# A decoder trunk on one core: turning the second layer's x token-major by transposing transfers of 16-bit halves

## The chip, the core and the metric

The kernel runs on one core of a Trainium2 chip. The core has five engines with in-order instruction queues: TensorE (PE, matrix products; its weight loads are shown apart as PEld), VectorE (DVE), ScalarE (ACT), GpSimd (POOL) and SyncE (SP), which here only issues transfers. Transfers run on 16 DMA engines, whichever queue issues them. The metric is the device time of one execution in microseconds; the smaller, the better.

## The reference

Two layers of a hybrid decoder trunk on x of shape (1, 512, 1024) in float32. Each layer adds two terms to x: the mixer (four gated branches, merged and projected by `w_out`) and a gated feed-forward network.

```
h = rmsnorm(x, norm_mix)
... four branches from h @ w_in, lifted, gated and summed: merged
x = x + merged @ w_out
hf = rmsnorm(x, norm_ffn)
gate, up = split(hf @ ffn_w_up, 2)
x = x + (silu(gate) * up) @ ffn_w_down
```

The change concerns the third line of the second layer. There x must exist in two layouts: with features on the partitions, for the products with `ffn_w_up`, and with tokens on the partitions, because the second layer's feed-forward output is accumulated onto x in that layout and written out.

## The kernel before

x lies feature-major: `xT` is a tile of 128 partitions x 8 feature chunks x 512 tokens. Every product is made from float32 values split into a high and a low part (`w_hi`, `w_lo`; `h_hi`, `h_lo`; `mg_hi`, `mg_lo`): three matmuls, at lines 320, 321 and 323, take the place of one. SP loads a piece of weights into `w_raw` (four buffers), ACT makes `w_hi` from it (three buffers, line 100, the helper `A` through which all ACT work goes), DVE makes `w_lo` (lines 257 and 1265). A matmul on a piece waits for both. A load is issued when a `w_raw` buffer is free.

`residual` (line 1178) forms `x + merged @ w_out`. It goes through the eight feature chunks m in four groups of two. In each group PE multiplies, and then for each m DVE adds the product to `xT[:, m, :]` (line 1193), `h_chunk` makes `h_hi`, `h_lo` and a square for the norm (lines 338 and 346 on DVE, line 100 on ACT), and the chunk is stored: in the first layer by a plain transfer of `xT` to `x_dram`, in the second layer by `turned(m)`. `turned` is the part that the change rewrites. Before, PE transposes four 128x128 blocks of the chunk into one PSUM tile `tr` (line 1181), ACT copies that tile to `xt` in SBUF, and a transfer on ACT's queue (line 1184) stores `xt` to `xt_dram` (`x_tokens` in the rows), which is laid out by tokens.

After `residual` comes `ffn`. Its first products, A11 and A12, take `h_hi` and `h_lo` directly. Line 1422 on DVE forms sums of them in a tile `acc`; a block of wide products follows (its loads at line 246). Then the accumulator `acc` is loaded by SP from `x_tokens` (`x_in`, line 1457), in two transfers, each after all stores to `x_tokens`. The last four PE transposes are kept in the list `last_turn`; `product` orders the second token tile's first matmul of A11 behind them.

The framework fixes the order of the instructions on each engine by a plan made before the run, in which urgent pieces (`w_hi`, `w_lo`) are taken first. On the chip each engine goes through its queue in that order and waits where an operand is not there yet. SBUF pools are freed and reused by tile: a later tile on the same place waits for the last user of the earlier one. `turned` takes its tiles from the pool `outp`, which holds `mg_hi`, `mg_lo` and two buffers of `xt`.

POOL meanwhile moves sums of the feed-forward weights through DRAM, one transfer after another (line 1280).

Of the kernel before, what the change touches and what calls it, by code (L numbers as in the profile page):

```python
# [12 lines left out]
F32 = mybir.dt.float32  # L13
F32R = mybir.dt.float32r
I32 = mybir.dt.int32
U8 = mybir.dt.uint8
AF = mybir.ActivationFunctionType
OP = mybir.AluOpType
AX = mybir.AxisListType
# [2 lines left out]
P = 128  # L22
S = 512
NT = S // P
# [47 lines left out]
def hybrid_trunk(ctx: ExitStack, tc: tile.TileContext, x, mem, positions, norm_mix, w_in, conv_w,  # L72
                 dsa_q_norm, dsa_k_norm, hgrn_lower_bounds, hgrn_out_norm, mem_norm, mem_w_kv,
                 mem_q_norm, mem_k_norm, w_lift, w_out, norm_ffn, ffn_w_up, ffn_w_down, out):
    nc = tc.nc
    act, dve, pe, pool = nc.scalar, nc.vector, nc.tensor, nc.gpsimd
# [11 lines left out]
    sync = mybir.DependencyInfo(mybir.DependencyClass.Sync, mybir.DependencyReason.DATA)  # L88
    tables = {AF.Exp: "natural_log_exp_and_others", AF.Ln: "natural_log_exp_and_others",
              AF.Silu: "silu_and_others"}  # L90
    table = {"set": None, "load": None, "users": []}

    def A(dst, src, func, **kw):
        name = tables.get(func)
        if name is not None and name != table["set"]:
            load = act.preload_act_table_set(name)
            for u in table["users"]:
                tc.add_manual_dep(load.ins, u.name, order, reason="table set")
            table.update(set=name, load=load.ins, users=[])
        i = act.activation(dst, src, func, **kw)  # L100
        if name is not None:
            tc.add_manual_dep(i.ins, table["load"].name, order, reason="table set")
            table["users"].append(i.ins)
        return i

    def mm_ps():
        return pmm.tile([P, 512], F32, name="mm")
# [4 lines left out]
    def tr_ps():  # L112
        return pat.tile([P, 512], F32, name="tr", bufs=TR_BUFS)

    def f(ap):
        return ap.bitcast(F32)

    consts.tile([P, 320], U8, name="spacer")
    ident = consts.tile([P, P], F32, name="ident")
# [17 lines left out]
                       base=0, channel_multiplier=1)  # L137
    future = consts.tile([P, P], U8, name="future")
    dve.tensor_scalar(future, causal_bias, 0.0, None, op0=OP.is_lt)
# [3 lines left out]
                       channel_multiplier=-1)  # L143
    tri = consts.tile([P, P], U8, name="tri")
    dve.tensor_copy(tri, tri_f)
    ps = tr_ps()
# [8 lines left out]
    warm = consts.tile([P, 1], F32, name="warm")  # L155
    A(warm, one, AF.Exp)
    mem_in = sp.tile([P, 2, D], F32, name="mem_in")
    for hf in range(2):
        c = slice(hf * D // 2, (hf + 1) * D // 2)
# [3 lines left out]
    ps = tr_ps()  # L163
    pe.transpose(ps[:, :KD], rows_m, ident[:KD, :KD])
    A(prm_m, ps[:, :KD], AF.Copy)
    N_ROWS = 70
    prm = consts.tile([P, N_ROWS], F32, name="prm")

    def parameters():
        ps = tr_ps()  # L170
        pe.transpose(ps[:, :N_ROWS], rows[:N_ROWS, :], ident[:N_ROWS, :N_ROWS])
        A(prm, ps[:, :N_ROWS], AF.Copy)

# [20 lines left out]
    for l in range(DEPTH):  # L194
        a = sp.tile([P, HD], F32, name=f"gq_raw{l}")
# [3 lines left out]
        b = consts.tile([P, HD], F32, name=f"gk{l}")  # L199
# [4 lines left out]
    def rstd(dst, ms, y, a):  # L204
        i = A(y, ms, AF.Ln, bias=eps[:, 0:1])
        A(y, y, AF.Exp, scale=-0.5, bias=half[:, 0:1])
        A(a, y, AF.Square, scale=2.0)
        dve.scalar_tensor_tensor(a, ms, EPS, a, op0=OP.add, op1=OP.mult)
        dve.scalar_tensor_tensor(dst, a, 3.0, y, op0=OP.subtract, op1=OP.mult, reverse0=True)
        return i  # L210
# [69 lines left out]
    def wchunk(src, kt, n):  # L280
        return Chunk(src, kt, n)
# [4 lines left out]
    def features(w, a, js, k0=0, kt=None, pss=None, made=None, late_lo=False):  # L286

        kt = w.kt if kt is None else kt
        pss = [mm_ps() for _ in js] if pss is None else pss
        runs = [(part, ks) for part in range(2) for ks, _, _ in w.parts] if late_lo else [(None, ks) for ks, _, _ in w.parts]  # L290
        for part, ks in runs:
            for j, ps in zip(js, pss):
                for k in ks:
                    last = mm3(ps, w.tile(k, j), pair(a, k0 + k), k0 + k == 0, k0 + k == kt - 1, part=part)[-1]
            if made is not None and (ks[-1] == w.kt - 1 or not late_lo):
                made.append(last)
        return pss
# [34 lines left out]
    def new_h():  # L332
        return (state.tile([P, KD, S], F32R, name="h_hi", bufs=1),
                state.tile([P, KD, S], F32R, name="h_lo", bufs=1))

    def h_chunk(h, ssq, c, gain, xs):
        A(h[0][:, c, :], xs, AF.Copy, scale=gain)
        dve.scalar_tensor_tensor(h[1][:, c, :], xs, gain, f(h[0][:, c, :]), op0=OP.mult, op1=OP.subtract)
        if ssq is None:
            return  # L340
        if c == 0:
            A(ssq, xs, AF.Square)
        else:
            sq = state.tile([P, S], F32, name="sq", bufs=2)
            A(sq, xs, AF.Square)
            dve.tensor_add(ssq, ssq, sq)
# [7 lines left out]
    def column_means(ps, ones, sq, hi, lo, scale=1.0):  # L354
        A(hi, sq, AF.Copy, scale=scale)
        dve.scalar_tensor_tensor(lo, sq, scale, f(hi), op0=OP.mult, op1=OP.subtract)
        return [pe.matmul(ps, ones, hi, start=True, stop=False), pe.matmul(ps, ones, lo, start=False, stop=True)]
# [3 lines left out]
    def norm_feature(ssq):  # L361
        ps = tr_ps()
        norm_mms.extend(column_means(ps, ones_hr, ssq, *(scratch512(S).bitcast(F32R) for _ in range(2)), scale=P / D))
        r = state.tile([P, S], F32, name="rstd", bufs=1)
        rstd(r, ps, scratch512(S), scratch512(S))
        return r
# [3 lines left out]
    def norm_token(ssq):  # L370
        ps = tr_ps()
        for t in range(NT):
            pe.matmul(ps[:, t:t + 1], ssq[:, t * P:(t + 1) * P], ones_d, start=True, stop=True)
        r = small(NT, name="rstd_t", bufs=2)
        after_split.append(rstd_into(r, ps[:, :NT], small, NT))
        return r
# [69 lines left out]
    h = new_h()  # L446
# [729 lines left out]
    last_turn = []  # L1176

    def residual(xT, w2d, a, kt, cols, h2, ssq2, gain, turn=None):
        def turned(m):
            ps = tr_ps()  # L1180
            last_turn[:] = [pe.transpose(ps[:, t * P:(t + 1) * P], xT[:, m, t * P:(t + 1) * P], ident) for t in range(NT)]
            xt = turn.tile([P, NT, P], F32, name="xt", bufs=2)
            A(xt, ps.rearrange("p (a b) -> p a b", b=P), AF.Copy)
            nc.scalar.dma_start(xt_dram[:, :, m * P:(m + 1) * P], xt)

        for m0 in range(0, KD, cols // P):
            w = wchunk(w2d[:, m0 * P:m0 * P + cols], kt, cols)
            pss = [mm_ps() for _ in range(cols // P)]
            for js in ([range(cols // P)] if m0 + cols // P < KD else [[j] for j in range(cols // P)]):
                features(w, a, js, 0, kt, [pss[j] for j in js])  # L1190
            for j in range(cols // P):
                m = m0 + j
                dve.tensor_add(xT[:, m, :], xT[:, m, :], pss[j])
                h_chunk(h2, ssq2, m, gain(m), xT[:, m, :])
                if turn is None:
                    nc.scalar.dma_start(x_dram[:, m, :], xT[:, m, :])
                else:
                    turned(m)
# [430 lines left out]
    for l in range(DEPTH):  # L1629
        with ExitStack() as ctx_mix:  # L1630
            h, ssq = mixer(l, h, (lambda: (norm_token(ssq), lambda: norm_feature(ssq))) if l else (lambda: norms), ctx_mix)
        h, ssq = ffn(l, h, ssq)
# [29 lines left out]
```

## Time and profile before

| | us |
|---|---|
| median of 3 runs | 1971.31 |
| lowest and highest run | 1971.04 and 1971.98 |
| span of the profiled execution, first to last instruction | 1969.1 |
| PE busy in that span | 1962.7 |
| stretch from the first chunk's addition of `residual` in the second layer (1598.78) to the last (1634.26) | 35.48 |

The profiled execution has no time of its own beside its span; 2.2 us of the median lie outside the span. PE's share of the span is 100%, and its granted clock is 2.4 GHz throughout (1.000 of full speed). DVE is busy for 75% and ACT for 60% of the span. An engine's busy time counts overlapped work of PE once; a matmul's duration runs from its start to its modelled end, while the next one has already started.

### The profile page before, as it was taken

To read this page: it belongs to the slowest core of one execution; us is meant where nothing else is said; L and a number is where in the kernel's file an instruction comes from. 1 tells how busy PE (TensorE), PEld (TensorE's weight loads), DVE (VectorE), ACT (ScalarE), POOL (GpSimd) and SP (SyncE) were. 2 spreads that over 40 slices of the span, in tenths; PEclk is the share of its full clock that TensorE was granted. 3 is DMA by queue.
4 is the path that set the end of the run, shared out by engine and by line. 5 is a ranking of instruction groups with operands and counts; after the bars stand their busy time and mean duration, and the time that the engine had idled before them with its cause. 6 is when DMAs were issued, how large, how long until landed. Compare 5 with 4: busy or idle time off the path is not lost.

```text
span 1969.1 us, 27206 instructions
## 1 busy us (share of the span) xinstructions
PE 1962.7 (100%) x9815; PEld 1646.4 (84%) x9815; DVE 1477.5 (75%) x2761; ACT 1182.0 (60%) x2038; POOL 235.6 (12%) x288
## 2 busy tenths in 40 slices
PE   9999999999999999999999999999999999999999
PEld 8898988878888888888889898888888888888887
DVE  7869997657776677776876889965678667867777
ACT  6653655866765456645655455477667656556464
POOL 1011111111111111100001111111111111111000
PEclk9999999999999999999999999999999999999999
DMA  8677667667777888886676766676677879888754
GB/s 303 204 173 172 166 166 173 154 146 173 170 190 207 226 234 266 241 237 191 198 223 162 177 150 168 160 181 152 165 176 171 210 196 253 254 263 239 213 185 138
DMA packets 224278, 385.27 MB, mean 196 GB/s; under 512 B 13194, under 2 KB 120272, under 8 KB 223888
## 3 DMA queue, kind: packets, MB, share of 16 engines
q1 hardware_dynamic: 165056, 244.16, 39.4%
q0 software_dynamic: 52192, 132.81, 32.9%
q10 hardware_dynamic: 6896, 6.58, 1.0%
q8 instruction: 77, 1.26, 0.2%
q14 instruction: 57, 0.47, 0.1%
HBM read 368.81 MB, written 140.51 MB: 259 GB/s over the span
## 4 chain that ended last, share of the span: by engine, by line
PE 100%; DVE 0%; ACT 0%; issue 0%; DVEq 0%; ACTq 0%
PE mm L320 24%; PE mm L321 24%; PE mm L323 24%; PE at L323 4%; PE at L320 4%; PE at L321 4%; PE tr L320 2%; PE tr L323 1%; PE tr L321 1%; PE at L838 1%; PE tr L878 1%; PE tr L867 1%; PE tr L1554 1%; PE at L837 1%; PE tr L804 0%; PE at L1136 0%
## 5 line engine op out<-in xcount | busy, mean ns | idle before, releaser
L100 ACT ACTIVATE w_hi<-w_raw 128x1024 fp32r<-128x1024 f32 (+1 forms) x435 | 457.5, 1054 | 350.8 <-PE mm L321 108.9
L320 PE MATMUL mm<-h_hi,w_hi 128*128 128x512 f32 x960 | 376.8, 394 | 0.0
L321 PE MATMUL mm<-h_lo,w_hi 128*128 128x512 f32 x960 | 376.8, 392 | 0.0
L323 PE MATMUL mm<-h_hi,w_lo 128*128 128x512 f32 x960 | 372.0, 393 | 0.0
L1265 DVE TENSOR_TENSOR w_lo<-w_raw,w_hi 128x1024 fp32r<-128x1024 f32 x211 | 256.2, 1217 | 130.1 <-ACT w_hi L100 129.3
L257 DVE TENSOR_TENSOR w_lo<-w_raw,w_hi 128x1024 fp32r<-128x1024 f32 (+1 forms) x224 | 272.0, 1216 | 78.6 <-ACT w_hi L100 76.7
L1280 POOL DMA_DIRECT2D up_sums<-in_ffn_w_up_dram x120 | 121.4, 1011 | 834.3 <-DMA up_sums<-in_ffn_w_up_dram 549.6
L320 PEld LDWEIGHTS mm<-h_hi,w_hi 128*128 128x128 f32 x960 | 180.4, 188 | 36.3 <-DVE zf L1053 0.8
L323 PEld LDWEIGHTS mm<-h_hi,w_lo 128*128 128x128 f32 x960 | 180.2, 188 | 36.3 <-issue 0.2
L321 PEld LDWEIGHTS mm<-h_lo,w_hi 128*128 128x128 f32 x960 | 180.4, 188 | 36.0
L321 PE MATMUL mm<-w_lo,h_hi 128*128 128x256 f32 (+2 forms) x568 | 187.6, 330 | 0.3 <-DVE w_lo L257 0.3
L323 PE MATMUL mm<-w_hi,h_lo 128*128 128x256 f32 (+2 forms) x568 | 187.7, 331 | 0.0
L320 PE MATMUL mm<-w_hi,h_hi 128*128 128x256 f32 (+2 forms) x568 | 181.4, 330 | 0.0
L321 PEld LDWEIGHTS mm<-w_lo,h_hi 128*128 128x128 f32 x568 | 107.7, 190 | 10.5 <-DVE w_lo L257 0.6
L323 PEld LDWEIGHTS mm<-w_hi,h_lo 128*128 128x128 f32 x568 | 107.7, 190 | 9.4
L320 PEld LDWEIGHTS mm<-w_hi,h_hi 128*128 128x128 f32 x568 | 107.4, 190 | 9.6 <-ACT w_hi L100 0.2
L1280 POOL DMA_DIRECT2D w_sums<-in_ffn_w_down_dram x66 | 62.2, 943 | 327.1 <-DMA w_sums<-in_ffn_w_down_dram 184.4
L100 ACT ACTIVATE prob<-prob,small 128x128 f32<-128x128 f32 (+3 forms) x128 | 68.8, 555 | 21.9 <-DVE small L853 16.3
L321 PE MATMUL mm<-y_lo,w_hi 128*128 128x512 f32 x192 | 75.7, 394 | 0.0
L320 PE MATMUL mm<-y_hi,w_hi 128*128 128x512 f32 x192 | 75.6, 395 | 0.0
L323 PE MATMUL mm<-y_hi,w_lo 128*128 128x512 f32 x192 | 75.3, 392 | 0.0
L100 ACT ACTIVATE gate_e<-gate 128x512 f32<-128x512 f32 x64 | 40.2, 628 | 41.9 <-DVE gate L661 41.3
(500 smaller groups left out, 4216.8 us busy)
## 6 DMA issues: line engine op xcount, KB each, us to landing
w_raw<-in_w_in_dram SPq DMA_DIRECT2D x144, 512.0 KB, 4.9
up_sums<-in_ffn_w_up_dram POOLq DMA_DIRECT2D x120, 512.0 KB, 7.0
w_raw<-up_sums SPq DMA_DIRECT2D x80, 512.0 KB, 5.1
w_raw<-in_ffn_w_up_dram SPq DMA_DIRECT2D x60, 512.0 KB, 4.8
w_sums<-in_ffn_w_down_dram POOLq DMA_DIRECT2D x54, 512.0 KB, 6.1
up_sums<-up_sums POOLq DMA_DIRECT2D x40, 512.0 KB, 5.0
w_raw<-in_w_lift_dram SPq DMA_DIRECT2D x32, 512.0 KB, 5.0
w_raw<-in_ffn_w_down_dram SPq DMA_DIRECT2D x24, 512.0 KB, 5.2
```

The lines of the kernel that those rows point to most:

```text
L100: i = act.activation(dst, src, func, **kw)
L257: i2 = dve.tensor_sub(lo, raw, f(hi))
L320: made += [pe.matmul(ps, ah, bh, start=first, stop=False, skip_group_check=more), pe.matmul(ps, ah, bl, start=False, stop=False, skip_grou ...
L321: pe.matmul(ps, ah, bl, start=False, stop=False, skip_group_check=more)]
L323: made += [pe.matmul(ps, al, bh, start=False, stop=last, skip_group_check=more)]
L837: return [pe.matmul(ps, q[:, hh, s], k[0][:, :n], start=True, stop=False), pe.matmul(ps, q[:, hh, s], k[1][:, :n], start=False, stop=True)]
L838: pe.matmul(ps, q[:, hh, s], k[1][:, :n], start=False, stop=True)]
L867: turn = pe.transpose(pp[:, (2 * e + i) * P:(2 * e + i + 1) * P], probs[2 * i + e][:, b * P:(b + 1) * P], ident)
L878: i = pe.matmul(pv[e * HD:(e + 1) * HD, c], vt[:, b, :], pt[:, b, e * 2 * P:(e + 1) * 2 * P], start=b == 0, stop=b == t)
L1265: two = A(hi, raw, AF.Copy), dve.tensor_sub(lo, raw, f(hi))
L1280: i = nc.gpsimd.dma_start(dst, src, **kw)
L1554: turns.extend(pe.transpose(ps[:, t * P:(t + 1) * P], us[t][:, j * P:(j + 1) * P], ident) for t in range(NT))
```

## The change

In the second layer's `residual`, the PE transposes and the copy out of PSUM go. In their place, for each chunk m:

- `halves_turned`: ACT copies the chunk, read as 16-bit numbers, into a tile `planes` so that all first halves of the 512 words lie ahead of all second halves (128 x 1024 numbers of 16 bits). Then SP issues one transposing transfer of `planes` (256 KB) into a tile `halves`, by blocks of 128 columns.
- `halves_joined`: ACT copies `halves` into `xt`, so that the two halves of each word lie together again (128 x 1024 numbers of 16 bits).

The store of `xt` on ACT's queue stays. `planes` and `halves` have two buffers of 2 KB per partition each, in the pool `outp`, which grows by 8 KB per partition. The list `last_turn` stays empty, so the order of A11's matmul behind the transposes goes too. Nothing else in the program is changed.

```diff
+    def halves_turned(src, planes, turned):
+
+        e = planes.bitcast(U16).rearrange("p (e c) -> p e c", e=2)
+        A(e, src.bitcast(U16).rearrange("p (c e) -> p e c", e=2), AF.Copy)
+        nc.sync.dma_start_transpose(turned.bitcast(U16).rearrange("p (b r) -> p b r", r=P), planes.bitcast(U16))
+
+    def halves_joined(dst, turned, blocks):
+
+        h = turned.bitcast(U16).rearrange("p (e b r) -> p e b r", e=2, r=P)[:, :, blocks, :]
+        A(dst.bitcast(U16).rearrange("p (b r e) -> p e b r", e=2, r=P), h, AF.Copy)
...
     def residual(xT, w2d, a, kt, cols, h2, ssq2, gain, turn=None):
         def turned(m):
-            ps = tr_ps()
-            last_turn[:] = [pe.transpose(ps[:, t * P:(t + 1) * P], xT[:, m, t * P:(t + 1) * P], ident) for t in range(NT)]
+            planes, halves = (turn.tile([P, S], F32, name=nm, bufs=2) for nm in ("planes", "halves"))
+            halves_turned(xT[:, m, :], planes, halves)
             xt = turn.tile([P, NT, P], F32, name="xt", bufs=2)
-            A(xt, ps.rearrange("p (a b) -> p a b", b=P), AF.Copy)
+            halves_joined(xt.rearrange("p a b -> p (a b)"), halves, slice(0, NT))
             nc.scalar.dma_start(xt_dram[:, :, m * P:(m + 1) * P], xt)
```

## Rows read from the trace of the kernel before

**Rows 1.** The page: span, busy time by engine, and chain by engine.
```profile
span 1969.1 us, 27206 instructions
...
PE 1962.7 (100%) x9815; PEld 1646.4 (84%) x9815; DVE 1477.5 (75%) x2761; ACT 1182.0 (60%) x2038; POOL 235.6 (12%) x288
...
PE 100%; DVE 0%; ACT 0%; issue 0%; DVEq 0%; ACTq 0%
```

**Rows 2.** All waits of PE, whole span: total us, times, longest us.
```profile
PE tr L148 <- DVE one L130: 1.2, 1, 1.2
PE mm L539 <- ACT w_hi L100: 0.7, 1, 0.7
PE mm L321 <- DVE w_lo L257: 0.3, 1, 0.3
```

**Rows 3.** Line 1181, the transposes: duration ns min/median/max, first and last start.
```profile
L1181 PE MATMUL tr<-ident,xT x32: 270/272/273, 1603.8 to 1637.6; 128*128 128x128 f32 x32
```

**Rows 4.** Timeline of PE around one chunk's transposes: start us, us, instruction.
```profile
1612.63 0.39 PE L321 MATMUL mm<-mg_lo,w_hi 128*128 128x512 f32 x1
1612.86 0.60 PE L1181 MATMUL tr<-ident,xT 128*128 128x128 f32 x4
...
1613.53 0.40 PE L320 MATMUL mm<-mg_hi,w_hi 128*128 128x512 f32 x1
```

**Rows 5.** Timeline of DVE: additions to x in layers one and two.
```profile
644.16 1.29 DVE L1193 TENSOR_TENSOR xT<-xT,mm 128x512 f32<-128x512 f32 x2 [3.35 <-PE mm L323]
...
1598.78 1.28 DVE L1193 TENSOR_TENSOR xT<-xT,mm 128x512 f32<-128x512 f32 x2 [3.35 <-PE mm L323]
...
1634.26 0.69 DVE L1193 TENSOR_TENSOR xT<-xT,mm 128x512 f32<-128x512 f32 x1 [0.63 <-PE mm L323]
```

**Rows 6.** Timeline of ACT: first evaluation of the wide block, layers one and two.
```profile
706.32 0.37 ACT L100 ACTIVATE fu<-at,rstd_t 128x128 f32<-128x128 f32 x1 [0.25 <-PE at L323]
...
1664.78 0.37 ACT L100 ACTIVATE fu<-at,rstd_t 128x128 f32<-128x128 f32 x1 [0.30 <-PE at L323]
```

**Rows 7.** Busy time between these marks: engines (instructions), clock, DMA share, GB/s.
```profile
644.16:706.32 62.16, 62.16 (x279) 51.57 (x278) 45.57 (x54) 34.58 (x45) 7.46 (x8) 1.00 0.86 229
1598.78:1664.78 66.00, 66.00 (x311) 54.76 (x310) 45.55 (x54) 39.05 (x53) 8.03 (x9) 1.00 0.87 230
```

**Rows 8.** Timeline of ACT at the end of the second layer's residual.
```profile
1637.89 0.60 ACT L100 ACTIVATE xt<-tr 128x512 f32<-128x512 f32 x1 [1.19 <-PE tr L1181]
...
1639.29 1.06 ACT L100 ACTIVATE w_hi<-w_raw 128x1024 fp32r<-128x1024 f32 x1 [0.79 <-PE mm L323]
```

**Rows 9.** Timeline of DVE behind that.
```profile
1640.38 1.23 DVE L1265 TENSOR_TENSOR w_lo<-w_raw,w_hi 128x1024 fp32r<-128x1024 f32 x1 [2.77 <-ACT w_hi L100]
1641.52 4.62 DVE L1422 TENSOR_TENSOR acc<-h_hi,h_lo 128x1024 f32<-128x1024 f32 x4
1646.06 1.22 DVE L257 TENSOR_TENSOR w_lo<-w_raw,w_hi 128x1024 fp32r<-128x1024 f32 x1
```

**Rows 10.** Timeline of PE: the matmul that uses this last low part.
```profile
1647.55 0.40 PE L321 MATMUL at<-w_lo,h_hi 128*128 128x512 f32 x1
```

**Rows 11.** Line 1184, the stores of xt: issue in ns; us from issue to landing.
```profile
L1184 ACTq DMA_DIRECT2D x_tokens<-xt x8: 520/521/669, 1605.1 to 1638.5; - x8
...
DMA to landing us min/median/max: 4.8/6.8/9.8
```

**Rows 12.** The page's DMA queues: packets, MB, share of 16 engines (q1 SP, q10 ACT).
```profile
q1 hardware_dynamic: 165056, 244.16, 39.4%
...
q10 hardware_dynamic: 6896, 6.58, 1.0%
```

**Rows 13.** Timeline of SP's queue: loads around the end of residual, accumulator load.
```profile
1633.65 3.78 SPq L246 DMA_DIRECT2D w_raw<-in_ffn_w_up_dram  x4
1637.54 1.47 SPq L1469 DMA_DIRECT2D w_raw<-up_sums  x2
...
1661.20 0.80 SPq L1457 DMA_DIRECT2D acc<-x_tokens  x2
```

**Rows 14.** The page's DMA issues: count, KB each, median us to landing.
```profile
w_raw<-in_w_in_dram SPq DMA_DIRECT2D x144, 512.0 KB, 4.9
```

## What I expect of the change

> **What bounds the kernel now.** I read the page first, then PE's waits, then the transposes themselves, then the stretch around them, and last the queues that the change adds work to. The page says that PE is busy for 1962.7 of 1969.1 us and that the chain that ended last is PE alone [rows 1]. A busy share can hide stalls, so the waits come next: in the whole span PE waits three times, 2.2 us together, none of them in the second layer's residual [rows 2]. PE's queue therefore sets the end. Work taken off PE is worth its slot in that queue, and work on another engine costs nothing until it holds a matmul back.
>
> **What the removed transposes cost.** There are 32 of 272 ns [rows 3]. Their sum, 8.7 us, is not what they cost, because a PE instruction starts before the one ahead has ended. The timeline shows the slot: from the start of one matmul at 1612.63 to the start of the one two further on at 1613.53 pass 0.90 us, four transposes included [rows 4]. Two matmul slots without them take 0.45 us (0.227 each, as 1612.63 to 1612.86 shows it to two digits), so four transposes take 0.45 us and 32 take 3.6.
>
> There is a better measure, because the first layer runs the same residual without turning. I take the same two marks in both layers, the addition of the first chunk [rows 5] and the first evaluation of the wide block in the feed-forward network [rows 6]. Between them lie 62.16 us in the first layer and 66.00 us in the second. The windows say what differs: PE has 279 instructions in one and 311 in the other, which is 32 more, DVE has 54 in both, ACT 45 and 53, which is the eight copies out of PSUM; clock and DMA share are alike [rows 7]. So the turning costs 66.00 - 62.16 = 3.84 us, 0.12 us for a transpose. That holds everything it does to PE, the slightly slower matmuls behind it too. I take 3.84 us as the gain, with 3.6 as its lower end. It is also the ceiling: PE doesn't wait in this stretch, so there is nothing else to win.
>
> **What the change adds on ACT.** For each chunk the copy out of PSUM (128x512, 0.60 us) becomes two copies of 128x1024 16-bit numbers. No row has 16-bit numbers. A copy of as many 32-bit elements takes 1.06 us [rows 8]; I take that, because the count of elements is the same. By bytes it would be 0.60, and if each strided half cost a whole access more, 2.1 us (an estimate, twice the row). So ACT gets 2 x 1.06 - 0.60 = 1.5 us more per chunk, 12.2 us in all (from 4.8 to 29). The stretch has 66.00 - 39.05 = 27 us of ACT idle time [rows 7], so the middle value fits; the cover is the `w_hi` pieces made ahead of PE. Where is that cover thin? At the end of the residual: the `w_hi` piece at 1639.29 sat 0.79 us waiting for PE [rows 8], the low parts follow on DVE behind 4.62 us of sums, the last ends at 1647.28 [rows 9], and a matmul that reads it starts at 1647.55 [rows 10]. ACT may be 0.79 + 0.27 = 1.06 us late there, which is just one copy. One copy in front of that piece costs nothing, two (a join of chunk 6 and a split of chunk 7, say) cost 1.06 us, of which I take half: 0.5 us, between 0 and 1.1.
>
> **What it adds on SP and the DMA engines.** Eight transposing transfers of 256 KB go into SP's queue, each behind ACT's first copy. Queued behind them on SP are weight loads, under 1 us of issue each (two in 1.47 us), with those of the wide block and of the next product right at the end of the stretch [rows 13]. A transfer waiting there for 1.06 us of ACT's copy is harmless: the loads are issued far ahead, and PE never waits for one. The join on ACT waits for the transfer, and behind it wait the next `w_hi` and, on ACT's queue, the store of `xt`.
>
> The trace has no transposing transfer, so I bound it. Below: moved as 128 rows of 2 KB at SP's mean of 16 x 1969.1 x 0.394 / 165056 = 75 ns for a packet, spread over 16 engines, 128 x 75 / 16 = 0.6 us of their time [rows 12]; eight of these are 5 us of DMA time in a stretch whose DMA engines are busy for 0.87 [rows 7]. Above: the slowest store of the same 256 KB lands after 9.8 us, the median one after 6.8 [rows 11]. Cut into 256-byte rows (one 128-column block), it would be 1024 x 75 / 16 = 4.8 us. I take a transfer that lands in about the 4.8 to 6.8 us of a plain one and lets the next overlap, since that row has the same bytes in the same stretch. The accumulator load at 1661.20 needs all stores of `x_tokens` [rows 13]. The last chunk's addition ends at 1634.95 [rows 5]; `h_hi`, the square and the split put the transfer at about 1637.4. With 6.8 us, a join of 1.06, an issue of 0.52 and a landing of 6.8 the last store is there at 1652.6, so 8.6 us remain. Buffers add 8 KB per partition; the three tiles have two buffers each, so at most two chunks are under way. The dropped order behind `last_turn` frees PE and costs nothing. DVE gets nothing.
>
> **Sum.** 3.84 gained, 0.5 lost: span 1969.1 - 3.3 = 1965.8. The 2.2 us outside the span stay, so from the median 1971.31 - 3.3 = 1968.0 us.
>
> **The rivals.**
>
> *ACT is held by a join, transfers overlapping.* The plan puts the last join at some place among the `w_hi` pieces; if the transfer then lands later than planned, ACT stands. If the whole landing time is exposed, ACT is held for 6.8 - 1.06 = 5.7 us beyond the slack, and the time is 1971.31 - 3.84 + 5.7 = 1973.2; with 9.8 us it is 1976.2. For it: the order on ACT is fixed beforehand and the slack is a single microsecond at the end. Against: within the residual a `w_out` piece feeds 24 matmuls (5.4 us), so the earlier joins have more room, and the plan does see a transfer's delay.
>
> *The transfers queue up one after another.* This is the slower side. The chunks arrive within 35.48 us [rows 5]. The first transfer can start at about 1603.5, where its predecessor's transposes stood [rows 3]. If each occupies its queue for t, the eighth ends at 1603.5 + 8t, against 1637.4 + t if it never waits. It is late by 7t - 33.9, so the point from which this decides is t = 4.8 us. The joins pass that on to ACT, and with 1.06 us of slack PE loses 7t - 35. At t = 6.8 that is 12.6 us, and the time 1971.31 - 3.84 + 12.6 = 1980.1; at 9.8 it is 33.6 us and 2001. For it: pieces of 256 bytes give 4.8 us by SP's row, on the very point. Against: the loads of 512 KB on this queue overlap and land after 4.9 us in the median [rows 14].
>
> The Trainium skill speaks against the change here. VectorE: DVE Perf Modes, section The three transpose paths, gives 1309 ns for a 128x128 block of 16 bits by the crossbar transfer, and its rules prefer TensorE where PSUM will do. Eight blocks one after another would be 10.5 us, an estimate from that page, and by the formula above 2006 us. DMA: Bandwidth & Descriptors, section Latency and other measured facts, gives 261 GB/s for a transposing transfer, which would be 1.0 us and leave the sum alone. No row here shows either.
>
> *A transpose is worth its duration.* 32 x 272 ns gives 1971.31 - 8.7 = 1962.6. For it speaks only the mean duration; the starts in [rows 4] and the comparison of the layers [rows 7] exclude most of it. The Trainium skill (TensorE: Matmul & The Clock Gate, Part 4: PE-mode transpose) gives about 275 ns in one kernel's context; the trace agrees with it as a duration, and shows 0.12 us as the slot.
>
> **How the numbers follow.** About 0.2% (3.9 us) is what a measurement of this kernel can tell from no change, and the ceiling of 3.84 us lies just under it. The forecast's case, a gain of 2.7 to 4, has 0.50; I count 0.13 of it as faster by over 0.2%, since its upper end touches that bound, and 0.37 as within. ACT held by a join: 0.17, of which 0.11 is within and 0.06 slower. Transfers one after another: 0.30, of which 0.28 is slower and 0.02 (t just at the point) within. The full duration: 0.03, faster. Together faster 0.16, within 0.50, slower 0.34. The forecast's own range is 1967.2 to 1968.7. The range starts at 1966.9 and reaches into the queueing case up to t = 7.9 us, 1971.31 - 3.84 + 7 x 7.9 - 35 = 1987.8, so 1988. Left out are the longer transfers (0.14) and the full gain (0.03).
>
> **What would show it.** Right: no line of transposes into `tr` in the residual, PE still without waits, and the marks of [rows 5] and [rows 6] 62 to 63 us apart in the second layer; ACT has 1.5 us more for each chunk; the transfers land within about 7 us. A wait of PE for `w_lo` or `w_hi` between 1634 and 1665, with ACT idle until a transfer, shows the first rival. Transfers landing later from chunk to chunk, with SP's loads behind them late, show the second. The forecast is wrong if a 16-bit copy costs much over 1.06 us, if a transfer holds SP's queue while it is made, or if transposing slows the other transfers.

## The result and the profile after

The changed kernel takes 1982.69 us in the median of 4 runs (1980.92 to 1984.57), against 1971.17 before: 11.5 us more, ratio 1.0059 with a 95% interval of 1.0044 to 1.0073. I had forecast 1968.0, a gain. The profiled execution of the changed kernel is the one of 1980.92 us, with a span of 1978.9.

The page of the changed kernel, where [rows 1] and [rows 12] stood before: PE has 32 instructions less and the same busy time, ACT 11 us more, and the chain that ended last has DMA, ACT and DVE in it, where it was PE alone.

```profile
span 1978.9 us, 27168 instructions
...
PE 1962.7 (99%) x9783; PEld 1643.6 (83%) x9783; DVE 1477.6 (75%) x2761; ACT 1193.2 (60%) x2046; POOL 235.6 (12%) x288
...
q1 hardware_dynamic: 173504, 246.25, 39.7%
...
PE 96%; DMA 2%; ACT 1%; DVE 1%; issue 0%; ACTq 0%; DVEq 0%
```

All waits of PE in the changed kernel (total us, times, longest), the answer to [rows 2]. The three waits of before are still there, 2.2 us together; 10.0 us are new, 8.5 of them for a `w_hi` from ACT.

```profile
PE mm L332 <- ACT w_hi L101: 6.9, 2, 6.2
PE at L332 <- ACT w_hi L101: 1.6, 1, 1.6
PE tr L160 <- DVE one L142: 1.2, 1, 1.2
PE at L333 <- DVE w_lo L269: 0.9, 2, 0.8
PE mm L551 <- ACT w_hi L101: 0.7, 1, 0.7
PE tr L385 <- DVE ssq L358: 0.6, 1, 0.6
PE mm L333 <- DVE w_lo L269: 0.3, 1, 0.3
```

The new operations of the changed kernel, by the tile `halves` and, in the second block, by the tile `planes` (ns min/median/max). ACT stood at the joins (`xt<-halves`) until a transfer had landed for 19.6 us in six cases. The transfers land after 5.5 us in the median. The landing does not grow from chunk to chunk: the first two took 5.0 and 5.2 us, the fourth 7.6, the next three 5.3 to 5.7, the last 7.8.

```profile
L123 SPq DMA_TRANSPOSE halves<-planes x8: 1232/1525/2333, 1602.0 to 1647.3; - x8
L101 ACT ACTIVATE xt<-halves x8: 1325/1364/1368, 1607.0 to 1655.1; 128x1024 uint16<-128x1024 uint16 x8
...
  ACT xt L101: 19.6, 6
...
DMA to landing us min/median/max: 5.0/5.5/7.8
```

```profile
L101 ACT ACTIVATE planes<-xT x8: 1039/1042/1045, 1600.9 to 1646.2; 128x1024 uint16<-128x1024 uint16 x8
```

The timeline of ACT in the changed kernel (start us, us, instruction, in brackets the idle time before it and its releaser). Read it as a queue: behind a first wait of 3.00 us, ACT stands 2.30 us for the join of one chunk, 3.04 for the next, 2.61 for the one after, and each time a `w_hi` piece comes out later.

```profile
1615.48 1.04 ACT L101 ACTIVATE planes<-xT 128x1024 uint16<-128x1024 uint16 x1
1618.82 1.37 ACT L101 ACTIVATE xt<-halves 128x1024 uint16<-128x1024 uint16 x1 [2.30 <-DMA halves<-planes]
1620.05 1.03 ACT L101 ACTIVATE w_hi<-w_raw 128x1024 fp32r<-128x1024 f32 x1
...
1624.13 1.37 ACT L101 ACTIVATE xt<-halves 128x1024 uint16<-128x1024 uint16 x1 [3.04 <-DMA halves<-planes]
...
1628.19 1.05 ACT L101 ACTIVATE w_hi<-w_raw 128x1024 fp32r<-128x1024 f32 x1
...
1633.93 1.34 ACT L101 ACTIVATE xt<-halves 128x1024 uint16<-128x1024 uint16 x1 [2.61 <-DMA halves<-planes]
...
1637.96 1.32 ACT L101 ACTIVATE xt<-halves 128x1024 uint16<-128x1024 uint16 x1
1639.16 1.03 ACT L101 ACTIVATE w_hi<-w_raw 128x1024 fp32r<-128x1024 f32 x1
```

The same three pieces of weights on ACT's timeline in the kernel before, which stand in the same order there. They were started at 1616.75, 1622.18 and 1631.31, so the delay grows from 3.3 to 6.0 to 7.9 us.

```profile
1616.75 1.05 ACT L100 ACTIVATE w_hi<-w_raw 128x1024 fp32r<-128x1024 f32 x1
...
1622.18 1.06 ACT L100 ACTIVATE w_hi<-w_raw 128x1024 fp32r<-128x1024 f32 x1 [0.52 <-PE mm L321]
...
1631.31 1.06 ACT L100 ACTIVATE w_hi<-w_raw 128x1024 fp32r<-128x1024 f32 x1 [0.54 <-PE mm L321]
```

Why it grows shows on DVE's timeline in the changed kernel. The last chunk's addition to x, which ended the residual at 1634.26 before [rows 5], starts at 1641.36, directly behind a low part that waited 2.25 us for the piece of 1639.16. Ahead of that, DVE stood 4.26 us for an `h_hi` that ACT made only behind the join of 1633.93. So a late join makes a late `h_hi` and a late `w_hi`, these make a late `h_lo` and a late `w_lo`, and these hold DVE's queue and with it the next chunk's addition, and from there the next split, transfer and join: the delay feeds itself.

```profile
1636.62 0.75 DVE L350 SCALAR_TENSOR_TENSOR h_lo<-xT,prm,h_hi 128x512 fp32r<-128x512 f32 x1 [4.26 <-ACT h_hi L101]
...
1640.22 1.23 DVE L1277 TENSOR_TENSOR w_lo<-w_raw,w_hi 128x1024 fp32r<-128x1024 f32 x1 [2.25 <-ACT w_hi L101]
1641.36 0.68 DVE L1205 TENSOR_TENSOR xT<-xT,mm 128x512 f32<-128x512 f32 x1
```

Busy time in the changed kernel around PE's longest wait (PE, PEld, DVE, ACT, POOL with instructions, then granted clock, DMA share, GB/s). PE stands 6.17 us, and the granted clock, 0.75 in the mean of that stretch, falls while it stands; in the 3.56 us behind it the clock is 0.50 (1.2 GHz). PE starts seven matmuls in these 3.56 us; the eighth, which the row counts too, starts at their end. At the 0.227 us a slot of [rows 4] seven would be 1.6 us, so the stall costs another 2.0 us.

```profile
1634.07:1640.24 6.17, 0.00 (x0) 0.00 (x1) 1.37 (x3) 5.57 (x7) 0.55 (x1) 0.75 0.82 235
1640.24:1643.80 3.56, 3.52 (x8) 2.34 (x8) 2.94 (x3) 0.90 (x1) 0.00 (x0) 0.50 0.96 245
```

PE's timeline there shows that the clock is not all of it. From 1642.09 to 1643.80 four slots take 0.43 us each, 0.2 more than at the full clock; for seven that is 1.4 us, an estimate. Most of the other 0.6 us is the gap ahead of 1641.50: that matmul reads the low part that DVE makes from the same late piece, from 1640.22 to 1641.45.

```profile
1640.24 1.22 PE L332 MATMUL mm<-w_hi,h_hi 128*128 128x512 f32 x2 [6.17 <-ACT w_hi L101]
1641.50 0.80 PE L333 MATMUL mm<-w_lo,h_hi 128*128 128x512 f32 x1
1642.09 0.63 PE L335 MATMUL mm<-w_hi,h_lo 128*128 128x512 f32 x1
...
1643.80 0.50 PE L333 MATMUL mm<-w_lo,h_hi 128*128 128x512 f32 x1
```

### The profile page after: what moved, and what is told of

Its sections match the earlier page's. It is cut to its first block, busy times and chain, and to the rows that moved or that the text cites. A ratio compares the mean times of both kernels' runs of the same rounds, so it can differ in the third digit from the quotient of the medians.

```text
span 1978.9 us, 27168 instructions
## 1 busy us (share of the span) xinstructions
PE 1962.7 (99%) x9783; PEld 1643.6 (83%) x9783; DVE 1477.6 (75%) x2761; ACT 1193.2 (60%) x2046; POOL 235.6 (12%) x288
## 3 DMA queue, kind: packets, MB, share of 16 engines
q1 hardware_dynamic: 173504, 246.25, 39.7%
## 4 chain that ended last, share of the span: by engine, by line
PE 96%; DMA 2%; ACT 1%; DVE 1%; issue 0%; ACTq 0%; DVEq 0%
PE mm L332 24%; PE mm L333 24%; PE mm L335 24%; PE at L333 4%; PE at L335 4%; PE at L332 4%; DMA halves<-planes 2%; PE tr L335 1%; PE tr L332 1%; PE tr L333 1%; PE at L850 1%; PE tr L890 1%; PE tr L879 1%; PE tr L1566 1%; PE at L849 1%
## 5 line engine op out<-in xcount | busy, mean ns | idle before, releaser
L333 PEld LDWEIGHTS mm<-w_lo,h_hi 128*128 128x128 f32 x568 | 108.1, 190 | 11.3 <-DVE w_lo L1277 0.8
```

What stands on the lines that cost most here:

```text
L333: pe.matmul(ps, ah, bl, start=False, stop=False, skip_group_check=more)]
```

## The experiments

Theory A: ACT works its queue in order and stands at a join until that chunk's transfer has landed; the weight pieces queued behind it reach PE late. Rivals: SP's queue is held by transfers that wait for ACT (S), the added work on ACT (W), the transfers slow the other transfers (D).

### The removed part alone

```diff
-            planes, halves = (turn.tile([P, S], F32, name=nm, bufs=2) for nm in ("planes", "halves"))
-            halves_turned(xT[:, m, :], planes, halves)
...
-            halves_joined(xt.rearrange("p a b -> p (a b)"), halves, slice(0, NT))
+            A(xt.rearrange("p a b -> p (a b)"), xT[:, m, :], AF.Copy)
```

> The kernel before with the 32 PE transposes of the second layer's residual taken out and nothing put in their place: ACT copies the chunk of xT as it stands (128x512) into xt, and the store stays, so the tokens' layout is left out and the output is not the reference's. This measures the removed part alone. My comparison of the two layers gives 3.84 us less, 1967.3 us; by the slots of four transposes it would be 3.6 us less, 1967.6; by the mean duration of a transpose 8.7 us less, 1962.5.

Measured: 1967.62 us against 1971.33, ratio 0.9982 (0.9974 to 0.9991), and PE waits as before the change. The transposes are worth 3.7 us, as the comparison of the two layers said. The 8.7 us of the mean duration are excluded.

### The join without its wait

```diff
-            halves_joined(xt.rearrange("p a b -> p (a b)"), halves, slice(0, NT))
+            halves_joined(xt.rearrange("p a b -> p (a b)"), planes, slice(0, NT))
```

> The changed kernel, but the joining copy on ACT reads planes, which ACT itself has just written, in place of halves, so it never waits for the transfer. ACT makes the same sixteen copies, SP issues the same eight transposing transfers and they move the same bytes; the turning is left out of the output. Theory A (ACT, in order, stands at a join until its transfer lands, and the weight pieces behind it come late to PE): 1967.3 to 1969.5 us, PE without waits in the residual. Theory S (SP is held by transfers that wait for ACT, and weight loads come late): about 1980 us. Theory W (the added work on ACT): about 1982 us, as the changed kernel. Theory D (the transfers slow the other transfers): about 1980 us.

Measured: 1967.23 us, ratio 0.9987 (0.9978 to 0.9996). Its waits of PE are the three of before, nothing else. The tile `halves`, in the second block, shows the same eight transfers, which land later than in the changed kernel, 7.6 us in the median:

```profile
PE tr L160 <- DVE one L142: 1.2, 1, 1.2
PE mm L551 <- ACT w_hi L101: 0.7, 1, 0.7
PE mm L333 <- DVE w_lo L269: 0.3, 1, 0.3
```

```profile
L123 SPq DMA_TRANSPOSE halves<-planes x8: 1243/1380/2811, 1602.4 to 1636.6; - x8
...
DMA to landing us min/median/max: 5.5/7.6/8.7
```

The plan puts the joins at partly other places on ACT here. With the same copies, the same transfers and the same bytes, the whole loss in the median is gone once no join waits for its transfer. S, W and D fall as causes of it.

### The same without the transfers

```diff
-        nc.sync.dma_start_transpose(turned.bitcast(U16).rearrange("p (b r) -> p b r", r=P), planes.bitcast(U16))
```

This on top of the edit before it.

> As the run before it, with the eight transposing transfers left out too; ACT's sixteen copies stay, the turning is left out of the output. Theory A: the same as with the transfers, 1967.3 to 1969 us, as nothing waited for them. Theories S and D: 1967.3 to 1969 us here, against some 1980 with the transfers. Theory W: still about 1982 us.

Measured: 1967.33 us, ratio 0.9980 (0.9972 to 0.9989). The median is the same as with the transfers: as long as no join waits for them, they cost nothing that shows in it, and neither do ACT's sixteen copies. Single executions differ: with the transfers, three of ten took 1971.0 to 1972.8 us; without them none of ten took over 1968.6. So the transfers may well cost some 4 us now and then by another path than a join that waits for them. That is argued from so few executions and not shown, and the path stays open, since no profile of a long execution of the kernel with the ready join was taken.

### Each join later on the queue

```diff
+            split_copy.append(halves_turned(xT[:, m, :], planes, halves))
+            waiting.append((m, halves))
+            if m >= 2:
+                joined(*waiting.pop(0), split_copy[-1])
...
+            i = halves_joined(xt.rearrange("p a b -> p (a b)"), halves, slice(0, NT))
+            if earlier is not None:
+                tc.add_manual_dep(i.ins, earlier.ins.name, order, reason="transfer first")
+            else:
+                late.append((len(hi_log) + {6: 3, 7: 6}[m], i))
```

`split_copy` holds the splitting copies; `late` puts the last two joins behind the third and the sixth `w_hi` that follow. `planes` and `halves` have three buffers in place of two, so that more chunks can be under way.

> The changed kernel with the whole computation, but each join is put later on ACT's queue: the join of chunk m behind the splitting copy of chunk m+2, the last two behind weight pieces of the feed-forward network (the third and the sixth). planes and halves have three buffers. Theory A: the transfers have landed by then, the waits go, 1967.5 to 1971 us. Theories S, W and D: no better than the changed kernel, about 1982 us, since the same work and the same transfers are there.

Measured: 1967.60 us against 1971.33, ratio 0.9986 (0.9978 to 0.9995), in 12 runs from 1966.55 to 1974.49. This is the whole computation, and by these runs faster than the kernel before. On ACT's timeline each of the first six joins now follows the split of a later chunk without standing; the last two stand 2.7 us together, for stores of `xt` and not for transfers into `halves`. The piece that came at 1639.16 in the changed kernel comes at 1630.27:

```profile
1623.88 1.04 ACT L101 ACTIVATE planes<-xT 128x1024 uint16<-128x1024 uint16 x1
1624.82 1.36 ACT L101 ACTIVATE xt<-halves 128x1024 uint16<-128x1024 uint16 x1
...
1630.27 1.03 ACT L101 ACTIVATE w_hi<-w_raw 128x1024 fp32r<-128x1024 f32 x1
```

### A plain transfer in the same place

```diff
-        nc.sync.dma_start_transpose(turned.bitcast(U16).rearrange("p (b r) -> p b r", r=P), planes.bitcast(U16))
+        nc.sync.dma_start(turned.bitcast(U16), planes.bitcast(U16))
```

> The changed kernel with a plain transfer of the same 256 KB from planes to halves in place of the transposing one, so the tokens' layout is left out. The order on ACT is instruction for instruction that of the changed kernel, and SP's too. If the trouble is that a transposing transfer takes long (5.5 us in the median there), a plain one lands after about 3 us, the joins wait less, and the time falls to 1968 to 1973 us. If a plain one takes as long in this stretch, as the stores of the same size do (6.2 us in the median), the trouble is any transfer between two steps of ACT, and the time stays at 1980 to 1985 us.

Measured: 1978.21 us, ratio 1.0036 (1.0025 to 1.0047), so between the two expectations and nearer to the second. The tile `halves` in this kernel, in the profile of its fastest execution (1975.16 us):

```profile
L123 SPq DMA_DIRECT2D halves<-planes x8: 465/468/620, 1602.0 to 1643.2; - x8
...
  ACT xt L101: 13.7, 5
...
DMA to landing us min/median/max: 2.7/4.9/7.2
```

A plain transfer lands 0.6 us earlier in the median (4.9 for 5.5) and is issued in 0.47 us where the transposing one took 1.53, and ACT still stands 13.7 us. Against the kernel with all joins later (1967.60) the changed kernel is some 15 us slower. Turning on the way accounts for some 4.5 of them (1982.69 less 1978.21, medians of 4 and 7 runs); the rest is the round trip over a transfer between two steps of one engine.

### The first six joins later, or the last two

Both are edits of the kernel with all joins later and keep its three buffers.

```diff
-            else:
-                late.append((len(hi_log) + {6: 3, 7: 6}[m], i))
```

for the first six later (the last two where the plan puts them), and, for the other,

```diff
-            if m >= 2:
-                joined(*waiting.pop(0), split_copy[-1])
+            if m < 6:
+                joined(*waiting.pop(0), ())
```

with the ordering of the first six left out.

> The whole computation; the joins of chunks 0 to 5 stand behind the splitting copy of the chunk two further on, the last two joins where the plan puts them; three buffers. The prediction held that only the last joins can hurt, as the weight pieces have more room before: by that the time would stay near 1980 us. The trace of the changed kernel shows PE standing 6.2 us ahead of 1640.2, behind the joins of chunks 3 to 5: by that this stall goes, the later ones of 3 us together stay, and the time is 1969 to 1972 us.

> The whole computation; the joins of chunks 0 to 5 where the plan puts them, the last two behind the third and the sixth weight piece of the feed-forward network; three buffers. By the prediction's step (only the last joins hurt) about 1968 us. By the trace of the changed kernel the stall of 6.2 us and some 2 us of lower clock behind it stay, and the time is 1975 to 1980 us.

Measured: 1971.85 us with the first six later, ratio 1.0002 (0.9990 to 1.0015), in 10 runs from 1966.63 to 1977.27; 1978.38 us with the last two later, ratio 1.0042 (1.0026 to 1.0059). The waits of PE, first those of the kernel with the first six later, then the long one of the kernel with the last two later:

```profile
PE mm L341 <- ACT w_hi L101: 2.7, 1, 2.7
```

```profile
PE mm L341 <- ACT w_hi L101: 6.2, 1, 6.2
```

So the earlier joins make the stall of 6.2 us: it stays with the last two later. With the first six later it is gone, the wait of 2.7 us that is left has another reason (see below), and the median is 10.8 us under that of the changed kernel. Putting the last two later is worth 4.3 us. The prediction's step, by which only the last could hurt, is shown wrong. The third buffer is not what helps, since the kernel with the last two later has it too and loses 7 us against the kernel before.

### What is left with all joins later

In the profile with the first six later, an execution of 1973.59 us, the last two joins did not stand for their transfers. ACT stood there 7.4 us until a store of `xt` had landed, because `xt` has two buffers, and PE's wait of 2.7 us is for a `w_hi` directly behind the first of these two joins. The first join stood 3.2 us for its transfer. I parted the same 12 buffers otherwise and ran the kernel with all joins later once more beside it.

```diff
-            planes, halves = (turn.tile([P, S], F32, name=nm, bufs=3) for nm in ("planes", "halves"))
+            planes, halves = (turn.tile([P, S], F32, name=nm, bufs=n) for nm, n in (("planes", 2), ("halves", 3)))
...
-            xt = turn.tile([P, NT, P], F32, name="xt", bufs=2)
+            xt = turn.tile([P, NT, P], F32, name="xt", bufs=3)
```

> The whole computation with all joins later, and the same 12 buffers of 2 KB parted otherwise: planes two, halves three, xt three (there three, three and two). ACT's order is the same instruction for instruction. With two buffers of xt a join also waited for the store of the chunk two before it (2.7 us in the profile of that kernel, 7.4 us with only the first six joins later), and single executions were 4 to 7 us longer. If that wait is what is left, the single long executions go and the median stays at 1967 to 1968 us. If they come from the transfers into halves, they stay.

> The kernel with all joins later and two buffers of xt once more, beside the one with three on the same chip: median 1967.5 to 1968 us, with one in six executions 4 to 7 us longer.

Measured, both on one chip: with three buffers of `xt` 1968.54 us, ratio 0.9989 (0.9980 to 0.9998), 11 runs from 1966.91 to 1973.60; with two 1968.96 us, ratio 0.9993 (0.9983 to 1.0003), 11 runs from 1966.69 to 1976.18. In the profile with three, no join waits for anything and PE has only the waits of before. In the profile with two, an execution of 1971.28 us, the joins stood for stores and for a transfer, and PE for 1.9 us:

```profile
ACT xt L101 <- DMA x_tokens<-xt: 4.5, 2, 2.7
...
ACT xt L101 <- DMA halves<-planes: 2.8, 1, 2.8
```

The wait for stores is part of what is left, but long executions stay with three buffers too, so the expectation that they would go is not borne out. Two long executions of kernels with the first six joins later were profiled, this one and the one of 1973.59 us, and in both the first two transfers into `halves` landed after 10.4 to 11.3 us. In the changed kernel they took 5.0 and 5.2. In the profiles of two short executions with all joins later (1967.44 us with two buffers of `xt`, 1967.21 with three) the first took 5.3 and 5.1 us and the second 9.1 and 8.4. All transfers into `halves` in the execution of 1971.28 us; the longest landing is that of the second:

```profile
L123 SPq DMA_TRANSPOSE halves<-planes x8: 1232/1330/2908, 1601.7 to 1637.5; - x8
...
DMA to landing us min/median/max: 3.7/6.9/10.9
```

A late first transfer so goes with these long executions, and the ten executions of the kernel without transfers have no long one. Whether late transfers are the cause with three buffers too is not shown, since no profile of a long execution with three buffers was taken; why they land late stays open.

The version with three buffers is faster than the kernel before by 0.02 to 0.20%; with two, the interval of this second measurement reaches 1.0003.

## Why the prediction was wrong, step by step

**The bound and the removed work: right.** PE set the end, and its transposes were worth 3.7 us where I had 3.84. The method carried: compare two stretches of one trace that differ in the thing alone.

**The copies: nearly right.** The split took 1.04 us (I had 1.06). The join took 1.36, so ACT got 1.8 us more per chunk and not 1.5. With 0.5 us for collisions the step was on the safe side: without waits all sixteen copies cost nothing that shows.

**The transfer: right in its landing.** It landed after 5.5 us in the median, within the 4.8 to 6.8 I took (the fourth and the last took 7.6 and 7.8), and the second was issued at 1604.1, before the first had landed. The upper bound's picture of 256-byte pieces is what the page shows, 173504 - 165056 = 8448 packets for eight transfers, 1056 each; but they are cheap. The queue's share grew by 0.397 x 1978.9 - 0.394 x 1969.1 = 10 us of 16 engines, an estimated 1.2 us for a transfer. That is rough, as the queue's time moves by some 4 us between kernels without any such transfer (39.4% of 1969.1 us before, 39.7% of 1964.8 with nothing turned), but far from the 8 x 4.8 = 38 us of my upper bound. The second rival, transfers one after another, did not happen: landing times don't grow from chunk to chunk, and the transfers of the kernel whose joins don't wait, which landed after 7.6 us in the median, cost nothing in its median. My range held the time by luck, only because that rival had widened it.

The Trainium skill (Advanced Engine Details and Errata, X-Bar Transpose (TRN2)) says that transposing transfers are as fast as regular ones. In their landing the runs nearly agree, 5.5 us against 4.9; in the issue on SP they don't, 1.53 against 0.47 us. Eight blocks at the 1309 ns of VectorE: DVE Perf Modes (The three transpose paths) would be 10.5 us, an estimate from that page; the longest landing in the changed kernel was 7.8.

**The join's wait: wrong, and this decided.** I saw it as the first rival, gave it 0.17, and priced it at the last join alone, 5.7 us less the gain, since "within the residual a `w_out` piece feeds 24 matmuls (5.4 us), so the earlier joins have more room". Two things were missed. I compared one wait with one piece's room, but the same queue holds eight joins, and a wait used up at one isn't given back before the next: three waits of 2.3 to 3.0 us in a row had moved a piece by 7.9 us, where I had put the slack at the end of this queue at 1.06 us in all [rows 8 to 10]. And I had not followed the wait past ACT, to DVE, where the next chunk's addition stands behind the late low parts, so that later transfers start late as well. "The plan does see a transfer's delay" did not help either: ACT stood at six of the eight joins, so the plan had left less work between split and join than the transfer takes.

**The end.** A stall also has a second price that I had left out: behind the longest one PE ran at 1.2 GHz and waited for the low part, 2.0 us together. Against the span of the kernel with nothing turned (1964.8), the changed kernel's 1978.9 is 14.1 us more. Waits of PE are 10.0 of it, the stretch behind the longest one 2.0. The waits are counted from the modelled end of the matmul before, 0.39 us after its start, where a slot is 0.227; by that the six new waits hold some 1.0 us more, an estimate. 1.1 us I can't place.

## What to carry to other kernels

When work is moved from a saturated engine to a route through other engines, ask for each step of the route what is queued behind it on its engine and how long it stands, and add the waits of all its repetitions along that queue. A step that waits for a transfer belongs on the queue where the transfer has landed, two chunks later and not one; here that order, with the third buffer that it needs, made 14 to 15 us, from 11.5 us more than before to 2.3 to 3.7 us less in the median. Two chunks were not always enough: where the first transfers landed after over 10 us, a join stood again. Idle time summed over a stretch is no cover for an in-order engine.

## What the runs showed of the hardware

A copy on ACT of 128x1024 16-bit numbers took 1.04 us where it reads with a stride and writes dense, and 1.36 us where it reads dense and writes with a stride; 32-bit numbers of the same count took 1.06. In the changed kernel the issue of a transposing transfer held SP for 1.23 to 2.33 us; that of a plain one of the same bytes took 0.47 in the median. The first two transposing transfers landed after 5.0 and 5.2 us in the changed kernel and after 10.4 and 10.9 in an execution of the kernel with all joins later. PE's granted clock was 0.50 (1.2 GHz) in the 3.56 us after it had stood for 6.17 us. And a 128x128 transpose of 32-bit numbers that lasts 272 ns [rows 3] takes only 0.12 us of PE's queue (3.7 us for 32).
